# Row gathers held back at layer boundaries and in the closing of the hybrid recurrences, with changed weaving rates

## The chip, the cores and the metric

The kernel runs on one core of a Trainium2 chip. The metric is the device time of one execution in microseconds. A core has five engines with an instruction queue each, which work side by side and wait for each other through semaphores: PE (TensorE, matrix products and transposes), DVE (VectorE), ACT (ScalarE), POOL (GpSimd) and SP (SyncE, which issues transfers). Each engine runs its own instructions strictly in order, so an instruction that waits holds up all that stand behind it in its queue.

## What is computed

A block of a language model for 512 tokens of width 1024, in float32: a Mamba-2 layer, a layer of sliding-window attention with sinks, a hybrid mixer (a gated delta rule and an mLSTM, four heads each), cross attention to 256 memory tokens, and a feed-forward part that gives each token 128 of 16384 small experts. Each layer normalises its input and adds its output. Cut to the layers' frame and to the feed-forward part, which the change is about:

```
x = x + rmsnorm(mamba2_mixer(rmsnorm(x, w0), ...), p0)
x = x + rmsnorm(swa_sink_mixer(rmsnorm(x, w1), ...), p1)
x = x + hybrid_mixer(rmsnorm_2(x, norm_mix_w), ...)
x = x + memory_cross_attention(rmsnorm_2(x, norm_xa_w), rmsnorm_2(mem, norm_mem_w), ...)
x = x + peer_ffn(rmsnorm_2(x, norm_ffn_w), ...)
return rmsnorm_2(x, norm_final_w)

# in peer_ffn, for a block of 128 tokens, after the choice of 8 x 16 experts eb with gates gb:
u = jnp.take(u_table, eb, axis=0)
act = gelu(jnp.einsum('phkd,pd->phk', u, xb))
out = jnp.einsum('phk,phkd->pd', gb * act, jnp.take(v_table, eb, axis=0))
```

The hybrid mixer ends with a normalisation of each head's output and a gate, and then the product with w_out:

```
go = rmsnorm_2(go, gdn_norm_w) * silu(g_z)
mh = rmsnorm_2(mh, mlstm_norm_w) * sigmoid(m_o)
return concatenate([go, mh]) @ w_out
```

## The kernel before

The 512 tokens are worked on in two groups of two blocks of 128. Each group runs through the five layers. The feed-forward part is done in two ways. The second group's goes through all experts as dense products: phase G builds a matrix of gates while the first products with U run, and phase D has 128 steps, one for each of 128 slices of the experts, of a product with U and one with V. The first group's feed-forward is done by rows: for each of its 2 blocks, each of 2 tables (u, then v) and each of 128 chosen experts, one indirect transfer fetches one row of 1024 numbers for each of the 128 tokens. That makes 512 gathers of 512 KB.

One such gather is issued by POOL (L1946). DVE then does one instruction with it: a dot product for a row of u (L1967), or a product and sum into x for a row of v (L1973). Between a block's last u and its first v come gelu on ACT (L1971) and a product with the gates on DVE (L1972). Six buffers `gu` hold rows, and `take` works on a row when five newer ones have been issued. After a block's last v row follows its final normalisation (`final`, L1856 to L1863, with the power `finr`).

These rows have no place of their own. The second group's layers are written as a generator that yields between pieces of work, and `run` issues rows at the yields (L1894 to L1905). At each yield a budget `acc` grows by a rate that belongs to the layer, never above 3; for each whole unit of it a row is issued, that is one gather and one DVE instruction for an older row. The rows get a lower priority by 300 places (GOFF) than the code around them, and a scheduler sorts each engine's instructions by priority and by when they can run; in the layers a row is also tied not to stand ahead of the matmul that was last written (`behind`). What is left of the rows when phase G ends is spread over the steps of phase D: a step gets a share of the rows left by its weight, 2 for the first 94 experts and 1 for the later ones.

The places around the change:

- A layer's last product is `out_part(..., last=True)` (L618). It works on four column pieces c of both blocks: c = 0, 1 of both, then c = 2, 3 block by block. Each piece is 8 matmuls; then `end_evac` adds it to the residual on DVE (L646), squares it on ACT (L648), and, where a norm follows the layer, multiplies it by a weight (L650, on DVE or POOL).
- `post` (L601) then makes the norm's factor: a reduction (L607), `rstd`, which is an addition on DVE (`pv`, L458) and a power on POOL (`pr`, L460), a product (L612) and the update of x in two halves (L615).
- `norm_T` (L480) makes the next layer's input: sums (L493 or L496), `rstd` again (`nv` L458, `nr` on POOL L460), the scaled x (`xn`, L500), PE transposes (`tp`, L412) and evacuations of these (L510). No product of the next layer can start before its first transposes.
- In the hybrid layer `finish(b, f0)` closes four heads of a block: ACT squares, DVE reduces (L1372 to L1374), `rstd` (`ov` L458, on POOL `or` L460), POOL multiplies with the gate (L1376), DVE with the factor (L1378). `outT` transposes the result. The heads f0 = 4 (mLSTM) are closed first, behind the recurrence; the heads f0 = 0 (gated delta rule) are woven into the first half of the product with w_out, whose evacuations are L656.
- `rstd`'s power runs on POOL, in the same queue as the gathers.

The matmuls of all layers stand at L404 in a helper. In the second group the boundaries lie, in the profiled execution, at 1106 to 1122 us (mamba to swa), 1266 to 1284 (swa to hybrid), 1538 to 1556 (hybrid to cross) and 1630 to 1640 (cross to route, the choice of experts); the closing in the hybrid layer at 1475 to 1525. Gates are built from 1825 to 1947, dense steps run from there to 2576.

Of the kernel before, what the change touches and what calls it, by code (L numbers as in the profile page):

```python
# [146 lines left out]
SPLIT_R = [V]  # L147
SPLIT_D = [V]
SPLIT = {"A": SPLIT_A, "B": SPLIT_B, "R": SPLIT_R, "D": SPLIT_D}
RB = 1.0  # L150
RR = 0.5
RT = 1.793
RBS = 1.1
RBH = 1.1
RBX = 1.1
RG = 0.5
RATE = {"A": 0.0, "T": RT, "B": RB, "R": RR, "G": RG, "swa": RBS, "hybrid": RBH, "cross": RBX}
RAWB = 3
# [17 lines left out]
class Cat:  # L176


    def __init__(self, tiles):
        self.tiles, self.n = tiles, tiles[0].shape[1]  # L180
# [6 lines left out]
class Kern:  # L187
    PD = 2

    def __init__(self, ctx, tc, a, out, groups, stop=None):  # L190
        self.ctx, self.tc, self.nc, self.a, self.out = ctx, tc, tc.nc, a, out
        self.groups = groups
        self.stop = stop
        self.cnt = {}
        pool = lambda n, b, **k: ctx.enter_context(tc.tile_pool(name=n, bufs=b, **k))
        self.cp = pool("c", 1)
        self.xp = pool("xp", len(groups))
        self.wp = pool("wp", 2)
        self.hp = pool("hp", 1)
        self.pp = pool("pp", 2)  # L200
        self.gp = pool("gp", 2)
        self.stack = {}
        self.phase = "A"
        self.tail = None
        self.rows = None
        self.hook = None
        self.tab = ("", [], [])
        self.push("op")
        self.push("cl")
        self.mp = pool("mp", 2, space=PSUM)  # L210
        self.dp = pool("dp", 2, space=DRAM)
        self.lp = None
        self.order, self.full = [], []
        for gi in range(len(groups)):
            w = weight_order(gi == 0)
            self.order += w
            self.full += [gi == len(groups) - 1 and PARTS.get(n[0]) in FULL for n in w]
        self.order += DENSE_SEQ
        self.full += [s[0] == "U" and s[1] < PLAIN for s in DENSE_SEQ]
        self.wraw, self.wsp = {}, {}  # L220
        self.wpos = self.rpos = self.cpos = 0
# [258 lines left out]
    def norm_T(self, x, nb, wcol, keep=None, halo=None, ss=None, full=False, dst=None):  # L480
        nc = self.nc
        gt = nb * 128
        xt = self.op_tile([128, nb, D], "xn", "oh") if "op" in self.stack else self.sb([128, nb, D], "xn", bufs=1)
        xn = [xt[:, b, :] for b in range(nb)]
        with self.tc.high_priority(HP):
            for b in range(nb):
                s4 = self.sb([128, 4], "nss")
                if ss is None:
                    for c in range(2):
                        sl = slice(512 * c, 512 * c + 512)  # L490
                        nc.scalar.activation(xn[b][:, sl], x[:, b, sl], AF.Square, accum_out=s4[:, c:c + 1])
                    s1 = self.sb([128, 1], "ns1")
                    nc.vector.tensor_tensor(s1, s4[:, 0:1], s4[:, 1:2], op=ALU.add)  # L493
                else:
                    s1 = self.sb([128, 1], "ns1")
                    nc.vector.tensor_reduce(s1, ss[:, b, :], axis=AX.X, op=ALU.add)  # L496
                r = self.rstd(s1, 1, "n", 1.0 / D)
                for c in range(2):
                    sl = slice(512 * c, 512 * c + 512)
                    nc.vector.tensor_scalar(xn[b][:, sl], x[:, b, sl], r, None, op0=ALU.mult)  # L500
        if dst is not None:
            hh, hl = dst
        else:
            hh, hl = self.hT_open(gt, halo, full)
        with self.tc.high_priority(HP):
            for k in range(8):
                p = self.ps([128, gt], "tp")
                for b in range(nb):
                    self.tr(p[:, b * 128:(b + 1) * 128], xn[b][:, k * 128:(k + 1) * 128])
                nc.scalar.activation(hh[:, k, :], p, AF.Copy, scale=wcol[:, k:k + 1])  # L510
                if full:
                    continue
                nc.vector.scalar_tensor_tensor(hl[:, k, :], p, wcol[:, k:k + 1], hh[:, k, :].bitcast(F32),
                                               op0=ALU.mult, op1=ALU.subtract)
        if keep is not None:
            for b in range(nb):
                nc.gpsimd.tensor_tensor(keep[0][:, b, :], xn[b], keep[1], op=ALU.mult)
        if halo is not None and halo[1] is not None:
            for j in range(2):
                nc.gpsimd.tensor_copy(halo[1][j], self.hx[j][:, :, gt:gt + 4])  # L520
        return hh, hl
# [96 lines left out]
    def out_part(self, key, oT, nb, kh, k0, evac, last=False, done=None):  # L618


        for c in (0, 1) if last else range(4):
            u = self.W((key, kh, c))
            for b in range(nb):
                p = self.ps([128, 256], "mm")
                self.n_half(p, u, oT, b, k0, True, True)
                evac(b, c, p)
                yield
        if last:
            us = [self.W((key, kh, c)) for c in (2, 3)]
            for b in range(nb):  # L630
                for c in (2, 3):
                    p = self.ps([128, 256], "mm")
                    self.n_half(p, us[c - 2], oT, b, k0, True, True)
                    evac(b, c, p)
                    yield
                if done is not None:
                    done(b)
# [403 lines left out]
    def hybrid(self, gi, x, nb):  # L1041
# [317 lines left out]
        oT = self.oT(gt, self.is_full(gi, "ho"))  # L1359

        def finish(b, f0):
            fs = slice(f0, f0 + 4)
            if f0 == 4:
                ab = self.sb([128, 4], "dab")
                nc.vector.scalar_tensor_tensor(ab, den[:, b], -1.0, den[:, b], op0=ALU.mult, op1=ALU.max)
                nc.vector.tensor_tensor(ab, ab, floor[:, b], op=ALU.max)
                nc.vector.reciprocal(cf[:, b, fs], ab)
            c = cf[:, b, fs]
            jk = self.sb([128, 4, 128], "sq", tag="X")
            so = self.sb([128, 4], "so")  # L1370
            nc.scalar.activation(jk, mixed[b][:, fs], AF.Square)
            nc.vector.tensor_reduce(so, jk, axis=AX.X, op=ALU.add)  # L1372
            nc.vector.tensor_tensor(so, so, c, op=ALU.mult)
            nc.vector.tensor_tensor(so, so, c, op=ALU.mult)  # L1374
            r = self.rstd(so, 4, "o", 1.0 / 128)
            nc.gpsimd.tensor_tensor(mixed[b][:, fs], mixed[b][:, fs], gate[:, b, fs], op=ALU.mult)  # L1376
            nc.vector.tensor_tensor(c, c, r, op=ALU.mult)
            nc.vector.tensor_tensor(mixed[b][:, fs], mixed[b][:, fs], c[:, :, None].to_broadcast([128, 4, 128]), op=ALU.mult)  # L1378
            yield

        def outT(f0):
            for f in range(f0, f0 + 4):
                self.to_T([mixed[b][:, f, :] for b in range(nb)], oT[0][:, f, :], self.lo(oT, f),
                          self.gdncol if f < 4 else self.mlcol[:, f - 4:f - 3])
                yield
# [7 lines left out]
        side = chain(*[gdn(b) for b in range(nb)])  # L1393
# [4 lines left out]
        yield from self.weave_keep(g_proj("h_z", 0, AF.Silu), side, 2.0)  # L1398
        yield from self.weave(side, ml, 0.5)
        yield from outT(4)  # L1400
        if gi == 0:
            yield from self.memory_kv(2, "cacc", 3)
        fin = chain(*[finish(b, 0) for b in range(nb)], outT(0))
        yield from self.weave(self.out_part("h_o", oT, nb, 1, 4, self.acc_evac(xs)), fin, 1.0)
        self.xss = self.pp.tile([128, nb, 4], F32, name="xss", tag="xss", bufs=2)
        yield from self.out_part("h_o", oT, nb, 0, 0, self.end_evac(xs, self.xss, "P"), last=True)
        if gi == 0:
# [478 lines left out]
    def run(self):  # L1886
# [4 lines left out]
        side = None  # L1891
        for gi, (b0, nb) in enumerate(self.groups):
            x = self.load_x(gi) if gi else x0
            acc = 0.0  # L1894
            for _ in self.layers(gi, x, nb):
                ph = "T" if self.tail is not None else self.phase
                if ph == "B" and self.layer in RATE:
                    ph = self.layer
                acc = min(3.0, acc + RATE[ph])
                while side is not None and acc >= 1:  # L1900
                    acc -= 1
                    with self.tc.high_priority(GOFF[self.phase] if self.tail is None else TOFF):
                        if next(side, 0) == 0:
                            side = None
# [8 lines left out]
            elif gi < len(self.groups) - 1:  # L1913
                side = self.after(gi, x, nb)
# [142 lines left out]
```

## Time and profile before

| | us |
|---|---|
| median of three executions | 2600.91 |
| the three | 2602.40, 2600.91, 2598.08 |
| the profiled execution, its own time | 2595.71 |
| its span in the profile | 2593.7 |
| PE busy | 2376.1 (92%) |
| DVE busy | 1987.4 (77%) |
| ACT busy | 1170.7 (45%) |
| POOL busy | 1077.3 (42%) |

The mean granted clock of the profiled execution is 0.963 of full speed. The page of the profile lists, in its section on the costliest groups, 256 gathers of u rows on POOL (313.0 us together) and 256 of v rows (367.5), 256 products L1967 on DVE (318.4) and 256 L1973 (335.3).

How to read it: a share of busy time is a mean over stages with different limits, so the stages are read one by one. Of a stretch, the table of busy times tells which engine has no free time in it. Where PE has gaps, the timeline of PE tells how long each gap was and what ended it, and the timelines of DVE and POOL tell what stood ahead of the instruction that PE waited for. A bracket such as `[3.27 <-POOL pr L460]` behind a row says that the engine stood idle for 3.27 us before it, and what ended that.

### The profile page before, as it was taken

Reading aid. Unit: us, or ns where it says so; the run is one execution under the profiler, and the core shown is the slowest. Engines: PE = TensorE matmul, PEld = TensorE weight load, DVE = VectorE, ACT = ScalarE, POOL = GpSimd, SP = SyncE. Lnnn points to the kernel's source line nnn. Section 1 sums busy time; section 2 is a strip of 40 time slices with the busy share of each in tenths; the row PEclk is TensorE's granted clock in tenths of the full one; section 3 lists DMA queues with packets and bytes.
Section 4 is the critical chain, followed back from the end, with each engine's and each line's share of the span. In section 5 each row is a group of like instructions: output and inputs, shape, how many; then the busy total and the mean of one; then the engine's idle time right before and its main releaser. Section 6 shows DMA issues by size and latency. Waiting matters only on the chain.

```text
span 2593.7 us, 41054 instructions
## 1 busy us (share of the span) xinstructions
PE 2376.1 (92%) x14872; PEld 2134.6 (82%) x14872; DVE 1987.4 (77%) x3989; ACT 1170.7 (45%) x2406; POOL 1077.3 (42%) x910
## 2 busy tenths in 40 slices
PE   7999998998989899979799859999769999999997
PEld 7999898998988788868678848888658999999974
DVE  7787657757589887877698786794997777777776
ACT  6766566644545433333252312222565444444443
POOL 1112001231011776753568775324335555555552
PEclk9999999999989899989899979999999999999999
DMA  6555434325446999986888689877888888888874
GB/s 203 178 172 156 148 118 142 116 89 150 141 131 197 352 380 358 341 297 224 336 308 302 226 324 353 288 236 282 249 237 302 316 311 286 319 317 300 294 276 152
DMA packets 203962, 642.33 MB, mean 248 GB/s; under 512 B 21104, under 2 KB 53360, under 8 KB 202480
## 3 DMA queue, kind: packets, MB, share of 16 engines
q1 hardware_dynamic: 97216, 347.19, 40.1%
q0 software_dynamic: 73728, 268.47, 28.6%
q10 hardware_dynamic: 32816, 24.06, 2.9%
q8 instruction: 117, 1.92, 0.3%
q14 instruction: 85, 0.70, 0.1%
HBM read 621.74 MB, written 17.89 MB: 247 GB/s over the span
## 4 chain that ended last, share of the span: by engine, by line
PE 60%; DVE 20%; issue 6%; POOL 6%; DMA 5%; ACT 4%; ACTq 0%; POOLq 0%; DVEq 0%; SPq 0%
PE mm L404 37%; PE ax L404 17%; PE tp L404 3%; POOL gu L1946 3%; PE tp L412 2%; DVE x L1973 2%; DVE gu L1967 2%; DMA gu<-in_p_v,eid 2%; DVE wlo L379 2%; DVE cacc L532 1%; DVE o L1736 1%; DMA gu<-in_p_u,eid 1%; DVE q L1738 1%; DVE o L1743 1%; ACT whi L376 1%
## 5 line engine op out<-in xcount | busy, mean ns | idle before, releaser
L379 DVE TENSOR_TENSOR wlo<-wraw,whi 128x1024 fp32r<-128x1024 f32 x285 | 357.2, 1254 | 206.7 <-ACT whi L376 206.4
L1946 POOL DMA_INDIRECT gu<-in_p_v,eid x256 | 367.5, 1436 | 192.4 <-DVE x L1973 111.5
L1946 POOL DMA_INDIRECT gu<-in_p_u,eid x256 | 313.0, 1223 | 273.8 <-DVE gu L1967 171.7
L404 PE MATMUL mm<-hl,whi 128*128 128x256 f32 (+1 forms) x1376 | 392.0, 285 | 0.0
L376 ACT CAST whi<-wraw 128x1024 fp32r<-128x1024 f32 x285 | 298.9, 1049 | 183.9 <-PE mm L404 86.6
L1967 DVE SCALAR_TENSOR_TENSOR gu<-gu,hf 128x1024 f32<-128x1024 f32 x256 | 318.4, 1257 | 45.4 <-DMA gu<-in_p_u,eid 45.0
L1973 DVE SCALAR_TENSOR_TENSOR x<-gu,act,x 128x1024 f32<-128x1024 f32 x256 | 335.3, 1310 | 14.4 <-DMA gu<-in_p_v,eid 13.4
L404 PE MATMUL mm<-hh,whi 128*128 128x260 f32 (+1 forms) x1232 | 331.9, 345 | 2.7 <-DVE spp L563 1.5
L404 PE MATMUL mm<-hh,wlo 128*128 128x260 f32 (+1 forms) x1200 | 320.9, 340 | 4.1 <-DVE wlo L379 4.1
L404 PEld LDWEIGHTS mm<-hl,whi 128*128 128x128 f32 x1376 | 262.7, 191 | 5.0
L1809 POOL TENSOR_TENSOR w<-act,w 128x256 fp32r<-128x256 f32 x128 | 146.4, 1144 | 281.9 <-issue 218.1
L404 PEld LDWEIGHTS mm<-hh,whi 128*128 128x128 f32 x1232 | 237.4, 195 | 22.7 <-ACT hh L510 2.8
L404 PEld LDWEIGHTS mm<-hh,wlo 128*128 128x128 f32 x1200 | 232.8, 196 | 21.5 <-DVE wlo L379 5.0
L404 PE MATMUL mm<-dhh,wlo 128*128 128x256 f32 x752 | 211.7, 282 | 0.0
L404 PE MATMUL mm<-dhh,whi 128*128 128x256 f32 x752 | 209.8, 279 | 0.0
L404 PE MATMUL mm<-wlo,hh 128*128 128x256 f32 x656 | 176.6, 329 | 0.0
L404 PE MATMUL mm<-whi,hh 128*128 128x256 f32 x608 | 166.8, 328 | 0.4 <-ACT hh L510 0.4
L404 PE MATMUL mm<-whi,oh 128*128 128x256 f32 x560 | 147.5, 328 | 1.3 <-DVE ysb L646 1.1
L404 PE MATMUL mm<-hh,wraw 128*128 128x256 f32 (+1 forms) x608 | 147.1, 390 | 0.3 <-ACT act L1706 0.3
L1804 ACT CAST w<-act 128x256 fp32r<-128x256 f32 x128 | 52.2, 408 | 206.9 <-DVE act L1802 204.7
L404 PEld LDWEIGHTS mm<-dhh,whi 128*128 128x128 f32 x752 | 141.1, 188 | 4.0
L404 PEld LDWEIGHTS mm<-dhh,wlo 128*128 128x128 f32 x752 | 141.3, 188 | 0.0
(494 smaller groups left out, 5646.6 us busy)
## 6 DMA issues: line engine op xcount, KB each, us to landing
wraw<-in_w SPq DMA_DIRECT2D x238, 512.0 KB, 4.0
wraw<-in_p_v SPq DMA_DIRECT2D x78, 512.0 KB, 4.7
wraw<-in_p_ut SPq DMA_DIRECT2D x69, 512.0 KB, 4.6
whi<-in_w SPq DMA_DIRECT2D x55, 512.0 KB, 6.1
wlo<-in_w SPq DMA_DIRECT2D x55, 512.0 KB, 6.2
wrawd<-in_p_v SPq DMA_DIRECT2D x50, 512.0 KB, 4.8
wrawd<-in_p_ut SPq DMA_DIRECT2D x36, 512.0 KB, 4.4
gd<-gst ACTq DMA_DIRECT2D x32, 384.0 KB, 3.6
```

Of the source, the lines that this page charges most:

```text
L376: nc.scalar.copy(hi, raw)
L379: (nc.gpsimd if le == "P" else nc.vector).tensor_tensor(lo, raw, hi.bitcast(F32), op=ALU.subtract)
L404: inst = self.last = self.nc.tensor.matmul(out, lhsT, rhs, start=start, stop=stop, skip_group_check=True)
L412: return self.nc.tensor.transpose(out, in_, self.ident[:in_.shape[0], :in_.shape[0]])
L532: nc.vector.scalar_tensor_tensor(acc, ps[:, 1 + j:1 + j + gt], w[:, j:j + 1], acc, op0=ALU.mult, op1=ALU.add)
L1736: nc.vector.tensor_tensor(o1, self.iota4.rearrange("p i t -> p t i"), row(self.sTb[:, 0, :]), op=ALU.is_equal)
L1738: nc.vector.tensor_tensor(q, self.iota4, col(self.sTb[:, 1, :]), op=ALU.is_equal)
L1804: nc.scalar.copy(wt[:, 0:gt], act)
L1809: nc.gpsimd.tensor_tensor(wt[:, gt:2 * gt], act, wt[:, 0:gt].bitcast(F32), op=ALU.subtract)
L1946: self.behind(k.nc.gpsimd.indirect_dma_start(out=t, out_offset=None, in_=table, in_offset=bass.IndirectOffsetOnAxis(ap=self.res[b][0][:, s ...
L1967: self.behind(nc.vector.scalar_tensor_tensor(t, t, 1.0, self.hf[:, b, :], op0=ALU.mult, op1=ALU.mult, accum_out=acts[b][:, s:s + 1]))
L1973: self.behind(nc.vector.scalar_tensor_tensor(x[:, b, :], t, acts[b][:, s:s + 1], x[:, b, :], op0=ALU.mult, op1=ALU.add))
```

## The change

It does two things. It changes the four rates: mamba 1.0 to 0.95, swa 1.1 to 1.15, hybrid 1.1 to 1.05, cross 1.1 to 0.95. And it adds a flag `quiet`. While it is set, `run` issues no row, except in the first group's tail (phase "T"). It is set when a layer's last product reaches its pieces c = 2, 3, and cleared when the next layer's `norm_T` has issued its transposes; it is set in the second group's `finish`, cleared after the transposes of the mLSTM half, set again by the `finish` of the other half and cleared when the first half of the product with w_out is written. The budget goes on growing meanwhile, up to its cap of 3. The flag stops rows from being issued into the program at these yields; rows issued at earlier yields keep the place that the scheduler finds for them.

```diff
-RB = 1.0
+RB = 0.95
-RBS = 1.1
-RBH = 1.1
-RBX = 1.1
+RBS = 1.15
+RBH = 1.05
+RBX = 0.95
...
         self.rows = None
+        self.quiet = False
... norm_T, behind the transposes and their evacuations
+        self.quiet = False
         if keep is not None:
... out_part
         if last:
             us = [self.W((key, kh, c)) for c in (2, 3)]
+            self.quiet = True
... hybrid
         def finish(b, f0):
+            self.quiet = gi > 0
             fs = slice(f0, f0 + 4)
...
         yield from outT(4)
+        self.quiet = False
...
         yield from self.weave(self.out_part("h_o", oT, nb, 1, 4, self.acc_evac(xs)), fin, 1.0)
+        self.quiet = False
... run
-                while side is not None and acc >= 1:
+                while side is not None and acc >= 1 and not (self.quiet and ph != "T"):
```

Rows issued in each stage of the second group, as the two programs issue them:

| stage | before | after |
|---|---|---|
| mamba | 126 | 116 |
| swa | 62 | 61 |
| hybrid | 109 | 91 |
| cross | 35 | 28 |
| route | 41 | 44 |
| phase G | 34 | 34 |
| phase D | 110 | 143 |

That is 36 rows fewer in the four layers. In phase D an expert of the first 94 gets 1.02 rows in the mean before and 1.32 after, a later one 0.51 and 0.66.

How the order on the engines changes is shown at three places. In the changed file the lines stand one to six higher: L1952 is L1946, L1973 is L1967, L653 is L650, L649 is L646, L461 is L460, L1380 is L1376. A row that ends in x4 stands for four alike.

POOL at the boundary mamba to swa, before, where `gu` is a row's gather, L650 a piece's weight and `pr` the norm's power:

```order
157 L460 TENSOR_TENSOR gr<-gv,mhalf 128x2
158 L1946 DMA gu<-in_p_u,eid 128x1024 x4
159 L650 TENSOR_TENSOR ysb<-ysb,bcw 128x256 x2
160 L1946 DMA gu<-in_p_u,eid 128x1024
161 L650 TENSOR_TENSOR ysb<-ysb,bcw 128x256
162 L1946 DMA gu<-in_p_u,eid 128x1024
163 L650 TENSOR_TENSOR ysb<-ysb,bcw 128x256
164 L1946 DMA gu<-in_p_u,eid 128x1024 x4
165 L460 TENSOR_TENSOR pr<-pv,mhalf 128x1 x2
```

And after:

```order
158 L461 TENSOR_TENSOR gr<-gv,mhalf 128x2
159 L1952 DMA gu<-in_p_u,eid 128x1024 x3
160 L653 TENSOR_TENSOR ysb<-ysb,bcw 128x256
161 L1952 DMA gu<-in_p_u,eid 128x1024
162 L653 TENSOR_TENSOR ysb<-ysb,bcw 128x256
163 L1952 DMA gu<-in_p_u,eid 128x1024
164 L653 TENSOR_TENSOR ysb<-ysb,bcw 128x256 x2
165 L461 TENSOR_TENSOR pr<-pv,mhalf 128x1 x2
```

The four gathers ahead of the two `pr` are gone, and none stands between the last two L650.

POOL in the closing of the hybrid layer, before, from the last factors of the recurrence (L1316, L1309) over the gate products (L1376) and the powers `or` of the two halves to the fourth `or`:

```order
260 L1316 TENSOR_TENSOR qd<-qd,cte 128x256 x2
261 L1309 TENSOR_TENSOR dec<-dec,triu 128x256
262 L460 TENSOR_TENSOR finr<-finv,mhalf 128x1
263 L1376 TENSOR_TENSOR mixed<-mixed,hgate 128x512
264 L1946 DMA gu<-in_p_u,eid 128x1024
265 L1376 TENSOR_TENSOR mixed<-mixed,hgate 128x512
266 L1946 DMA gu<-in_p_u,eid 128x1024
267 L1376 TENSOR_TENSOR mixed<-mixed,hgate 128x512
268 L460 TENSOR_TENSOR or<-ov,mhalf 128x4
269 L1946 DMA gu<-in_p_u,eid 128x1024
270 L1376 TENSOR_TENSOR mixed<-mixed,hgate 128x512
271 L1946 DMA gu<-in_p_u,eid 128x1024 x2
```

```order
272 L460 TENSOR_TENSOR or<-ov,mhalf 128x4 x2
273 L1946 DMA gu<-in_p_u,eid 128x1024 x4
274 L460 TENSOR_TENSOR or<-ov,mhalf 128x4
275 L1946 DMA gu<-in_p_u,eid 128x1024 x20
276 L460 TENSOR_TENSOR nr<-nv,mhalf 128x1 x2
```

The same place after:

```order
260 L1319 TENSOR_TENSOR qd<-qd,cte 128x256
261 L1380 TENSOR_TENSOR mixed<-mixed,hgate 128x512
262 L1952 DMA gu<-in_p_v,eid 128x1024 x2
263 L1380 TENSOR_TENSOR mixed<-mixed,hgate 128x512 x2
264 L1952 DMA gu<-in_p_v,eid 128x1024
265 L461 TENSOR_TENSOR or<-ov,mhalf 128x4
266 L1380 TENSOR_TENSOR mixed<-mixed,hgate 128x512
267 L1952 DMA gu<-in_p_u,eid 128x1024 x3
268 L461 TENSOR_TENSOR or<-ov,mhalf 128x4
269 L1952 DMA gu<-in_p_u,eid 128x1024 x2
270 L461 TENSOR_TENSOR finr<-finv,mhalf 128x1
271 L461 TENSOR_TENSOR or<-ov,mhalf 128x4 x2
```

Block 0's `finr` moves from ahead of the closing products to behind the second `or`; gathers still stand among the products, two, one, three and two of them.

DVE at the boundary hybrid to cross, before, where L646 is the evacuation of one piece, `gu,act` a row's product, and L496, L458, L500 lead to the next layer's transposes:

```order
1943 L1967 SCALAR_TENSOR_TENSOR gu,act<-gu,hf 128x1024
1944 L646 TENSOR_TENSOR x<-mm,x 128x256
1945 L1967 SCALAR_TENSOR_TENSOR gu,act<-gu,hf 128x1024
1946 L646 TENSOR_TENSOR x<-mm,x 128x256
1947 L1967 SCALAR_TENSOR_TENSOR gu,act<-gu,hf 128x1024
1948 L496 TENSOR_REDUCE ns_15326<-xss 128x1
1949 L496 TENSOR_REDUCE ns_15335<-xss 128x1
1950 L1967 SCALAR_TENSOR_TENSOR gu,act<-gu,hf 128x1024
1951 L458 TENSOR_SCALAR nv<-ns_15326 128x1
1952 L458 TENSOR_SCALAR nv<-ns_15335 128x1
1953 L1967 SCALAR_TENSOR_TENSOR gu,act<-gu,hf 128x1024
1954 L500 TENSOR_SCALAR xn<-x,nr 128x512 x4
```

And after:

```order
1916 L649 TENSOR_TENSOR x<-mm,x 128x256
1917 L1973 SCALAR_TENSOR_TENSOR gu,act<-gu,hf 128x1024
1918 L649 TENSOR_TENSOR x<-mm,x 128x256 x4
1919 L497 TENSOR_REDUCE ns_15239<-xss 128x1
1920 L497 TENSOR_REDUCE ns_15248<-xss 128x1
1921 L459 TENSOR_SCALAR nv<-ns_15239 128x1
1922 L459 TENSOR_SCALAR nv<-ns_15248 128x1
1923 L501 TENSOR_SCALAR xn<-x,nr 128x512 x4
```

The last four evacuations follow each other, and no row stands between them and the scaled x.

## Rows read from the trace of the kernel before

**Rows 1.** The page, busy time of each engine and its share of the span.

```profile
PE 2376.1 (92%) x14872; PEld 2134.6 (82%) x14872; DVE 1987.4 (77%) x3989; ACT 1170.7 (45%) x2406; POOL 1077.3 (42%) x910
```

**Rows 2.** Busy us by stretch: PE, PEld, DVE, ACT, POOL, then clock, DMA share, GB/s.

```profile
900.00:950.00 50.00, 45.82 (x218) 40.09 (x217) 41.15 (x80) 16.50 (x40) 38.76 (x30) 0.91 1.00 384
...
1110.00:1120.00 10.00, 0.00 (x0) 0.00 (x0) 4.94 (x22) 2.72 (x8) 4.68 (x8) 0.50 0.71 266
...
1540.00:1550.00 10.00, 5.71 (x18) 4.13 (x16) 9.12 (x20) 2.55 (x10) 4.68 (x5) 0.83 1.03 417
...
2200.00:2250.00 50.00, 50.00 (x324) 45.41 (x323) 39.89 (x37) 23.89 (x37) 26.54 (x19) 1.00 0.90 325
...
2500.00:2550.00 50.00, 48.09 (x183) 31.64 (x181) 37.01 (x39) 20.39 (x30) 25.39 (x21) 1.00 0.69 233
```

**Rows 3.** PE's timeline at the boundaries: start, duration, engine, line, operation, idle before it.

```profile
1120.04 0.66 PE L412 MATMUL tp<-ident,xn 128*128 128x128 f32 x2 [14.07 <-DVE xn L500]
...
1281.73 0.66 PE L412 MATMUL tp<-ident,xn 128*128 128x128 f32 x2 [13.72 <-DVE xn L500]
...
1542.20 3.36 PE L404 MATMUL mm<-wraw,oh 128*128 128x256 f32 x8 [1.90 <-DVE x L646]
...
1553.69 1.39 PE L412 MATMUL tp<-ident,xn 128*128 128x128 f32 x4 [6.08 <-DVE xn L500]
...
1628.34 1.89 PE L404 MATMUL mm<-whi,oh 128*128 128x256 f32 x8
...
1635.30 0.66 PE L412 MATMUL tp<-ident,xn 128*128 128x128 f32 x2 [3.34 <-DVE xn L500]
```

**Rows 4.** PE's waits from 1470 to 1525: sum, times, longest.

```profile
PE tp L412 <- DVE mixed L1378: 18.0, 2, 11.4
```

**Rows 5.** DVE's timeline in a dense step.

```profile
2200.26 1.23 DVE L379 TENSOR_TENSOR wlo<-wrawd,whi 128x1024 fp32r<-128x1024 f32 x1 [0.94 <-ACT whi L376]
...
2207.55 1.27 DVE L1973 SCALAR_TENSOR_TENSOR x<-gu,act,x 128x1024 f32<-128x1024 f32 x1
```

**Rows 6.** POOL's timeline at the boundary mamba to swa.

```profile
1106.54 0.99 POOL L1946 DMA_INDIRECT gu<-in_p_u,eid  x1 [0.16 <-issue]
...
1110.74 0.94 POOL L1946 DMA_INDIRECT gu<-in_p_u,eid  x1 [0.30 <-issue]
1111.70 0.59 POOL L460 TENSOR_TENSOR pr<-pv,mhalf 128x1 f32<-128x1 f32 x1
```

**Rows 7.** POOL's timeline in a dense step, one gather.

```profile
2203.94 1.77 POOL L1946 DMA_INDIRECT gu<-in_p_v,eid  x1
```

**Rows 8.** DVE's timeline at the boundary mamba to swa.

```profile
1107.11 0.14 DVE L458 TENSOR_SCALAR pv<-pss 128x1 f32<-128x1 f32 x1
...
1112.33 0.21 DVE L612 TENSOR_SCALAR pr<-pr,gr 128x1 f32<-128x1 f32 x1 [3.27 <-POOL pr L460]
```

**Rows 9.** POOL's timeline at the boundary swa to hybrid.

```profile
1268.18 1.73 POOL L650 TENSOR_TENSOR ysb<-ysb,bcw 128x256 f32<-128x256 f32 x1
...
1273.86 0.59 POOL L460 TENSOR_TENSOR pr<-pv,mhalf 128x1 f32<-128x1 f32 x1
```

**Rows 10.** DVE's timeline at the boundary swa to hybrid, the last row ahead of block 1's update.

```profile
1276.15 1.27 DVE L1973 SCALAR_TENSOR_TENSOR x<-gu,act,x 128x1024 f32<-128x1024 f32 x1
```

**Rows 11.** DVE's timeline at the boundary hybrid to cross.

```profile
1551.25 0.20 DVE L458 TENSOR_SCALAR nv<-ns 128x1 f32<-128x1 f32 x2
...
1553.06 1.67 DVE L500 TENSOR_SCALAR xn<-x,nr 128x512 f32<-128x512 f32 x4 [0.46 <-POOL nr L460]
```

**Rows 12.** DVE's timeline in route.

```profile
1651.09 0.49 DVE L1522 MAX8 tv<-sc 128x8 f32<-128x128 f32 x2 [11.25 <-ACT sc L1570]
```

**Rows 13.** PE's waits in mamba's body, 835 to 1100: sum, times, longest.

```profile
PE ax L404 <- DVE m_h L817: 14.4, 7, 4.8
```

**Rows 14.** PE's waits while gates are built, 1825 to 1950.

```profile
PE ax L404 <- DVE o L1743: 21.1, 18, 3.1
```

**Rows 15.** ACT's timeline in swa, at the first block's switch from u to v.

```profile
1133.38 1.28 ACT L1971 ACT_TABLE_LOAD   x1
```

## The prediction

> **What bounds the kernel now.** I read the busy shares first: PE works 92% of the span, the next engine 77% [rows 1]. So a gain can only come from stretches where PE stands, and the table of busy times by stretch says which those are [rows 2]. In the dense expert part PE is busy 50.00 of 50 us at full clock and DVE 39.89: PE sets the time there. In mamba PE is busy 45.82 of 50 with the granted clock at 0.91, and DVE is often what it waits for. At the boundary mamba to swa PE does nothing for ten microseconds, and the clock stands at 0.50, the lower of its two levels.
>
> Next I read, in PE's timeline, the row after each such gap [rows 3]. Its bracket tells how long PE stood and for which engine: 14.07 us at mamba to swa, 13.72 at swa to hybrid, 1.90 and then 6.08 at hybrid to cross, 3.34 at cross to route, all for DVE. Two waits of 18.0 us together end on DVE's L1378 in the hybrid closing [rows 4]. That is some 57 us at the places that the change touches. Much of it is a serial chain that no row gather causes (evacuate, square, reduce, power, scale, normalise, transpose); the question is what share of it is queued behind rows. The prices of a row are 1.27 us on DVE (its product) [rows 5] and 0.94 us on POOL alone, or 1.77 beside busy DVE, for its gather [rows 6, 7].
>
> **The change part by part.** Counting the gathers issued in each stage gives before and after: mamba 126 and 116, swa 62 and 61, hybrid 109 and 91, cross 35 and 28, route 41 and 44, gate building 34 and 34, dense 110 and 143. So 36 leave the four layers, 3 go to route and 33 to the dense part. The rows that the flag holds back are made up for by at most three afterwards, since the budget is capped at 3.
>
> *Mamba to swa.* POOL issues gathers from 1106.54 on, the last begins at 1110.74, and only then, at 1111.70, comes the power `pr` [rows 6]. Its input `pv` was written by DVE at 1107.11 to 1107.25, and DVE then stands 3.27 us for `pr` at L612 [rows 8]. The order of after has no gather ahead of `pr`, and none between the last two L650. POOL was free at 1106.38 (0.16 before its first gather), and `pv` comes by then, since the DVE row ahead of it is gone too. `pr` moves from 1111.70 to 1106.39: **5.3 us**. All behind it up to the transposes is a chain of the same pieces. Floor 3.3 (the wait at L612 alone), ceiling 6.6 (one more row of 1.27).
>
> *Swa to hybrid.* The last L650 on POOL ends at 1269.91, `pr` starts at 1273.86 behind three gathers [rows 9]: 3.95 us. A row of 1.27 us stands on DVE at 1276.15 between block 0's update and the transposes [rows 10]; it goes, while one evacuation, 0.33 us, moves in. 3.95 + 1.27 - 0.33 = **4.9 us**; floor 2.4, ceiling 6.5, if a second DVE row ahead also counted.
>
> *Hybrid closing.* Here flag and order disagree. The order of after shows eight gathers from the first closing product to the third `or`, where before there were five: rows generated earlier are placed late. Against that, block 0's final normalisation (its power `finr` and DVE's L1862) leaves the closing products and lands behind them. Following both orders by hand with the durations of before, the first transposes come about 1 us sooner, the second 2.9, and then PE stands 2.7 for block 0's other half. Of the 18.0 us of waits [rows 4] I take **1 us**; from -4 (three extra gathers of 1.3 us ahead of an `or`) to +4 (2.9 and 1 both kept).
>
> *Hybrid to cross.* Before, each of the last four L646 on DVE stands behind a row; after, the last four follow each other and L496, L458 and L500 stand directly behind. Three terms. PE's wait of 1.90 at 1542.20 for an L646 goes. The same eight matmuls took 3.36 us, where eight take 1.89 at full clock [rows 3]: 1.47. From the last matmul's end at 1547.61 to the transposes was 6.08; what stays is one evacuation and reduction (about 0.8), L458 to L500 by way of POOL (1553.06 - 1551.25 = 1.81, [rows 11]) and 0.63 to the transpose: 3.2, so 2.8 go. Sum **6.2 us**; floor 2.8, ceiling 8.
>
> *Cross to route.* Of the 3.34 us [rows 3], two rows sit between the last evacuations. The last matmul ends at 1631.96; without rows the normalisation of block 0 is out some 0.9 us later: **2.4 us**, from 0 to 3.3. The three rows that route gets fall into DVE's idle 11.25 us there [rows 12]: nothing.
>
> *Mamba's body.* Ten rows fewer, four of them at the boundary. PE waits 14.4 us, in seven pieces, for DVE's L817 [rows 13]. Six rows free 7.6 us of DVE; I take a quarter, **2 us**, since most rows lie beside PE work; from 0 to 7.6.
>
> *The switch of a block from u rows to v rows.* Block 1's leaves gate building, where it makes the longest of 18 waits, 3.1 us where the others average (21.1 - 3.1) / 17 = 1.1 [rows 14]: **2 us**. Block 0's moves in swa from the projections to directly ahead of the first softmax on ACT; its table load of 1.28 us [rows 15] plus 0.3 for the function then lie in that chain: **-1.6 us**, from -3 to 0.
>
> *The dense part.* 28 of the 33 rows go to its steady experts: 1.02 per expert before, 1.32 after. One expert takes 5.6 us. DVE idles 0.94 us in each ahead of one product, waiting for ACT [rows 5], and a row takes 1.27, so the average third of a row (0.4 us) fits. DVE runs ahead of PE by a ring of buffers, so an expert with two rows, which overshoots by 0.3 us, is smoothed over its neighbours. POOL is busy 26.5 of 50 us. The DMA share is 0.90 at 325 GB/s; 0.3 x 0.524 MB per 5.6 us adds 28 GB/s, and the boundary stretch of hybrid to cross shows 417 GB/s [rows 2]. So **0** there. In the tail of V products PE is busy only 48.09 of 50 [rows 2]; five rows there cost between 0 and 1.27 each, and I take 0.15: **-0.7 us**.
>
> A rule of the Trainium skill speaks against this part. In this trace a gather takes 1.77 us on POOL in the dense part and 0.94 where DVE stands [rows 7, 6]: it waits for DVE. The Trainium skill, "SBUF — State Buffer", section "Who interferes with whom", says why: VectorE and GpSimd share a port pair as an exclusive lock, so gathers whose descriptors GpSimd writes starve behind VectorE. That would make the dense part the worst place for more rows, and is the mechanism of the second rival below; the 1.77 agrees with it, but POOL still idles 23.5 of 50 us. By the rule the sum would be that rival's; by POOL's idle time it stays as it is.
>
> The sum: 5.3 + 4.9 + 1 + 6.2 + 2.4 + 2 + 2 - 1.6 - 0.7 = 21.5 us. The profiled run took 2595.71 us, so 2574.2 in its terms; the median of before, 2600.91, lies 5.2 above that run, which gives 2579.4, said as **2579**. The floors add up to 3.3 + 2.4 - 4 + 2.8 + 0 + 0 + 0 - 3 - 6.4 = -4.9, the ceilings to 6.6 + 6.5 + 4 + 8 + 3.3 + 7.6 + 2 = 38; all floors at once are unlikely.
>
> **The rivals.**
>
> *Given back.* The boundaries get shorter, but the next layer then starts while its weights or three catch-up rows still hold DVE or DMA (1.03 share at hybrid to cross, [rows 2]), and half or more of the gain is lost: 8 us left, 2593. For it: DVE rows in that stretch themselves wait for their data. Against it: the clock stands at its lower level in the gaps, and a shorter gap gives some of that back.
>
> *Slower: the moved rows cost their full price.* Place: the dense part's DVE, or POOL, whose gathers wait for DVE there. If DVE's lead over PE is eaten up and each of 33 rows costs 1.27 us, that is 42 - 21.5 = +20: 2621. It decides from 21.5 / 33 = 0.65 us a row on. Against it: DVE has 10 of 50 us free and PE none; a third of a row per expert needs 0.4 of 0.94.
>
> *Not what it says.* Rows are placed late by the scheduler, and as in the hybrid closing they may stay in the boundaries: 0 to 5 us, 2598. Against it: the orders of after show three of five boundaries clean.
>
> *More.* The layers may be bound throughout by DVE and DMA, as mamba looks; then each of the 36 rows taken out gives 1.27 us: 46 us, 2555. Against it: PE is at 10.00 of 10 in many stretches there.
>
> **How the numbers follow.** Forecast (gain of 8 to 37 us, around 2579) 0.67; given back 0.13; slower 0.06; not what it says 0.05; more 0.09. A measurement of this kernel can tell about 0.2%, 5.2 us, from no change: faster means below 2595.7, slower above 2606.1. "Given back" is faster in two of three cases. Faster 0.67 + 0.09 + 0.09 = 0.85; same 0.04 + 0.05 = 0.09; slower 0.06. The range 2563 to 2596 takes the ceilings' sum (2600.9 - 38) below and a gain of 5 us above; it leaves out the slower rival, most of "more" and part of "not what it says", together 0.17.
>
> **What would show each step.** In the profile of after: PE's gap ahead of the first transposes falls from 14.07 to about 9, from 13.72 to about 9, from 6.08 to about 3 and from 3.34 to about 1; POOL's `pr` starts within 0.2 us of its input; two waits on L1378 still add up to some 15 us; the dense part keeps PE at 50.00 of 50, with DVE near 43 and DMA near 350 GB/s. I am wrong if PE shows gaps in the dense part, if the gaps shrink but mamba, swa or hybrid between them grow, or if the gaps do not shrink at all.

## The result and the profile after

The changed kernel takes 2563.18 us (median of five, 2560.91 to 2571.5) against 2602.37 before (2598.08 to 2603.39): the ratio is 0.9857, with a 95% interval of 0.9838 to 0.9875. The forecast was 2579, with a range of 2563 to 2596. The direction is right and the time lies inside the range by 0.2 us, at its lower end, but the gain is 39 us where 22 were forecast. The profiled run took 2561.23 us, 34.5 less than the profiled run of before, where the sum said 21.5. So 13 us are to be accounted for.

First the rows that answer to [rows 3, 4]: PE's timeline of the changed kernel at the boundaries and in the closing (start, duration, instruction, idle time before it).

```profile
1105.18 0.66 PE L413 MATMUL tp<-ident,xn 128*128 128x128 f32 x2 [7.67 <-DVE xn L501]
...
1261.10 0.66 PE L413 MATMUL tp<-ident,xn 128*128 128x128 f32 x2 [7.57 <-DVE xn L501]
...
1481.30 0.69 PE L413 MATMUL tp<-ident,mixed 128*128 128x128 f32 x2 [12.06 <-DVE mixed L1382]
1486.89 0.66 PE L413 MATMUL tp<-ident,mixed 128*128 128x128 f32 x2 [4.89 <-DVE so L1378]
...
1499.65 0.41 PE L413 MATMUL tp<-ident,mixed 128*128 128x128 f32 x2 [1.08 <-DVE mixed L1382]
...
1523.74 0.41 PE L413 MATMUL tp<-ident,xn 128*128 128x128 f32 x2 [2.70 <-DVE xn L501]
...
1602.53 0.41 PE L413 MATMUL tp<-ident,xn 128*128 128x128 f32 x2 [1.00 <-DVE xn L501]
```

The gaps ahead of the four first transposes fell from 14.07, 13.72, 6.08 and 3.34 to 7.67, 7.57, 2.70 and 1.00. In the closing 12.06 + 4.89 + 1.08 stand where 11.41 + 6.55 stood: nothing gained there. No gather stands in the gap from mamba to swa any more, as POOL's timeline shows: `pr` now waits for its input and not for gathers (compare [rows 6]).

```profile
1092.10 0.98 POOL L1952 DMA_INDIRECT gu<-in_p_u,eid  x1 [0.16 <-issue]
1093.10 1.64 POOL L653 TENSOR_TENSOR ysb<-ysb,bcw 128x256 f32<-128x256 f32 x2
1095.48 0.57 POOL L461 TENSOR_TENSOR pr<-pv,mhalf 128x1 f32<-128x1 f32 x1 [0.74 <-DVE pv L459]
...
1102.35 0.75 POOL L916 MEMSET va<- 128x780 f32 x1 [1.82 <-DVE inv L875]
1103.05 0.61 POOL L918 COPY kT<-a_kc 128x512 f32<-128x512 f32 x1
1103.61 0.39 POOL L919 COPY va<-a_vc 128x260 f32<-128x260 f32 x1
1103.97 0.55 POOL L461 TENSOR_TENSOR nr<-nv,mhalf 128x1 f32<-128x1 f32 x1
```

What is left of that gap is not the bare chain. The input of `nr`, `nv`, is written at 1102.46 to 1102.61, and `nr` starts only at 1103.97, behind swa's own MEMSET and two copies. These 1.4 us stood there before the change too, and no row gather is their cause.

Then the dense part, busy us of PE, PEld, DVE, ACT, POOL, then granted clock, DMA share and GB/s of a stretch of the changed kernel. It answers to the fourth of [rows 2]: PE has no free time, DVE went from 39.89 to 42.84 and POOL from 26.54 to 32.42.

```profile
2200.00:2250.00 50.00, 50.00 (x324) 45.47 (x323) 42.84 (x40) 24.23 (x36) 32.42 (x21) 1.00 0.90 316
```

So the gaps shrank as forecast or more, except in the closing, and the dense part took the rows. The 13 us show when the span is cut at the same instructions in both traces. Durations in us; the number of gathers that POOL ran in each stretch stands behind a stroke.

| stretch, cut at PE's instructions | before | after | gained | in the sum |
|---|---|---|---|---|
| start to mamba's first `dtv` product | 806.1 | 804.4 | 1.6 | - |
| mamba's body | 299.9 / 122 | 293.1 / 116 | 6.8 | 2 |
| gap mamba to swa | 14.1 / 4 | 7.7 / 0 | 6.4 | 5.3 |
| swa | 148.0 / 58 | 148.3 / 61 | -0.4 | -1.6 |
| gap swa to hybrid | 13.7 / 5 | 7.6 / 0 | 6.2 | 4.9 |
| hybrid up to its closing | 209.0 / 75 | 208.1 / 76 | 0.9 | - |
| closing to cross's first transposes | 63.0 / 29 | 54.5 / 15 | 8.5 | 7.2 |
| cross to route's first transposes | 81.6 / 40 | 78.8 / 28 | 2.8 | 2.4 |
| route, gates, dense, end | 958.4 | 956.2 | 2.2 | 1.3 |

The four boundary stretches came in some 4 us above the sum altogether. The largest single difference is mamba's body, 4.8 us. Its two rows, before and after:

```profile
806.08:1105.97 299.89, 283.23 (x1432) 249.50 (x1432) 251.53 (x505) 117.72 (x278) 204.57 (x165) 0.94 0.91 335
```

```profile
804.44:1097.51 293.07, 275.73 (x1432) 244.13 (x1432) 249.45 (x493) 117.84 (x280) 192.90 (x160) 0.97 0.91 334
```

The same work, 1432 entries of PE, keeps it busy for 7.5 us less, at a mean granted clock of 0.97 where it was 0.94, and PE's idle time did not shrink (16.7 and 17.3 us). The DMA share is 0.91 in both.

### The profile page after: what moved, and what is told of

It is laid out like the page before. It is cut to its first block, busy times and chain, and to the rows that moved or that the text cites. A ratio compares the mean times of both kernels' runs of the same rounds, so it can differ in the third digit from the quotient of the medians.

```text
span 2558.7 us, 41068 instructions
## 1 busy us (share of the span) xinstructions
PE 2360.9 (92%) x14872; PEld 2124.7 (83%) x14872; DVE 1993.0 (78%) x3989; ACT 1169.8 (46%) x2406; POOL 1080.9 (42%) x910
## 4 chain that ended last, share of the span: by engine, by line
PE 62%; DVE 20%; issue 6%; POOL 5%; DMA 4%; ACT 3%; ACTq 0%; POOLq 0%; DVEq 0%; SPq 0%
PE mm L405 39%; PE ax L405 17%; PE tp L405 3%; PE tp L413 3%; POOL gu L1952 2%; DVE gu L1973 2%; DVE wlo L380 2%; DVE o L1742 1%; DMA gu<-in_p_v,eid 1%; DVE cacc L534 1%; DMA gu<-in_p_u,eid 1%; DVE x L1979 1%; ACT whi L377 1%; DVE o L1749 1%; DVE q L1744 1%
## 5 line engine op out<-in xcount | busy, mean ns | idle before, releaser
L380 DVE TENSOR_TENSOR wlo<-wraw,whi 128x1024 fp32r<-128x1024 f32 x285 | 355.0, 1247 | 175.3 <-ACT whi L377 174.6
L1952 POOL DMA_INDIRECT gu<-in_p_u,eid x256 | 315.6, 1233 | 332.3 <-DVE gu L1973 231.8
L1952 POOL DMA_INDIRECT gu<-in_p_v,eid x256 | 381.0, 1488 | 138.0 <-DVE x L1979 71.1
L1973 DVE SCALAR_TENSOR_TENSOR gu<-gu,hf 128x1024 f32<-128x1024 f32 x256 | 323.0, 1279 | 37.5 <-DMA gu<-in_p_u,eid 37.3
L1979 DVE SCALAR_TENSOR_TENSOR x<-gu,act,x 128x1024 f32<-128x1024 f32 x256 | 342.4, 1337 | 11.6 <-DMA gu<-in_p_v,eid 9.6
```

Of the source, the lines that this page charges most:

```text
L380: (nc.gpsimd if le == "P" else nc.vector).tensor_tensor(lo, raw, hi.bitcast(F32), op=ALU.subtract)
L1952: self.behind(k.nc.gpsimd.indirect_dma_start(out=t, out_offset=None, in_=table, in_offset=bass.IndirectOffsetOnAxis(ap=self.res[b][0][:, s ...
L1973: self.behind(nc.vector.scalar_tensor_tensor(t, t, 1.0, self.hf[:, b, :], op0=ALU.mult, op1=ALU.mult, accum_out=acts[b][:, s:s + 1]))
L1979: self.behind(nc.vector.scalar_tensor_tensor(x[:, b, :], t, acts[b][:, s:s + 1], x[:, b, :], op0=ALU.mult, op1=ALU.add))
```

## The experiments

The theory to be tested is the prediction's: the gain comes from the **places**, rows that stood ahead of the boundary chains. Its rival is the **count**: a row costs about the same wherever it stands in the layers, and 36 fewer at 39 / 36 = 1.08 us each are the gain. All ratios are against the kernel before, run on the same chip. RB, RBS, RBH and RBX are the rates of mamba, swa, hybrid and cross.

**Same counts, other places.** Two kernels separate them. In the first the flag is ignored and rates give the counts of after; in the second the flag works and rates give the counts of before.

```diff
-                while side is not None and acc >= 1 and not (self.quiet and ph != "T"):
+                while side is not None and acc >= 1:
... rates RB 0.92, RBS 1.09, RBH 0.92, RBX 0.88
```

> The flag is ignored and the rates are lowered further (0.92, 1.09, 0.92, 0.88), so that each layer has as many rows as the changed kernel (116, 61, 91, 29; dense 144) but rows stand in the boundaries as before. Theory 'places' (the gain comes from rows that no longer stand ahead of the boundary chains): the 14.07 and 13.72 us gaps stay, only mamba's 6.8 us and the switch's 2 us are gained, about 2593 us. Theory 'counts' (every row out of the layers gives its price of about 1.1 us back, wherever it stood: 36 x 1.08 = 39): about 2563 us, as the changed kernel.

Measured: 2569.80 us, ratio 0.9896 (0.9875 to 0.9917): 27 us gained by the ratio, without the flag. The first two gaps stayed at 11.7 and 13.6 us, and mamba's body alone gave 10.5.

```diff
-RB = 0.95, RBS = 1.15, RBH = 1.05, RBX = 0.95
+RB = 1.03, RBS = 1.17, RBH = 1.27, RBX = 1.20
```

> The flag works, and the rates are raised (1.03, 1.17, 1.27, 1.20), so that each layer has as many rows as the kernel before (126, 62, 108, 35; dense 108). Theory 'places': most of the gain stays, 39 less mamba's 6.8 and a little for denser rows between the boundaries, about 2575 us, with gaps of some 7.6 us at the first two boundaries. Theory 'counts': no gain, about 2602 us.

Measured: 2591.59 us, ratio 0.9967 (0.9950 to 0.9984): 9 us gained by the ratio, with the flag and no row fewer in the layers. Both theories missed, "places" by more: of the change's 37 us by its ratio some 27 go with the count and 9 with the places, and the two add up. Yet the gaps did shrink in the second kernel (8.3 and 9.0 us at the first two boundaries, 51.8 from the closing to cross, 77.6 in cross), by 5.8 + 4.7 + 11.1 + 4.0 = 26 us. Most of it was lost again in the bodies, to which the same rows had moved. (The profiled execution took 2597.61 us, 6 above the median; in it all of the 26 us was lost again.) Its hybrid body, and that of before:

```profile
1280.95:1507.14 226.19, 197.75 (x1080) 172.78 (x1080) 188.40 (x320) 69.85 (x152) 168.78 (x146) 0.93 0.83 293
```

```profile
1281.73:1490.74 209.01, 193.53 (x1080) 168.11 (x1080) 172.51 (x290) 75.19 (x156) 148.06 (x128) 0.95 0.79 274
```

Eighteen more rows there (93 for 75) cost 17.2 us, four more in mamba's body 7.8.

**The closing.** One kernel leaves the flag out of the hybrid closing, a second also lowers the hybrid rate so that the counts are those of after.

```diff
         def finish(b, f0):
-            self.quiet = gi > 0
... and in the second kernel
-RBH = 1.05
+RBH = 0.94
```

> The changed kernel without the flag in the hybrid closing; 10 rows return to the hybrid layer (101), dense 132. If the closing's part of the flag is worth what the two traces differ by there once the boundary to cross is taken off (9.1 - 0.65 - 6.2 = 2.3 us): about 2565 us. Theory 'counts': 10 x 1.08 = 11 us more, about 2574 us.

Measured: 2569.79 us, ratio 0.9883 (0.9863 to 0.9903): 7 us more than after by the ratio, but with 10 rows more in the layer, between the two expectations.

> The changed kernel without the flag in the hybrid closing, and the hybrid rate lowered to 0.94 so that the hybrid layer has 91 rows as in the changed kernel; all other counts are the same too. If only the count matters in the hybrid layer: 2563 us, as the changed kernel. If rows in the closing cost more than rows in the layer's body (the stretch from the closing to cross was 6.8 us longer without the flag): 2566 to 2570 us.

Measured: 2564.71 us, ratio 0.9874 (0.9857 to 0.9891), against 2562.44 for the changed kernel in the same session. Its stretch from the closing to cross takes 56.9 us with 21 rows, 3 us more than the 53.8 of the changed kernel there, but the times differ by 2.3 us, which lies within the intervals: that the flag in the closing is worth anything beyond its count is not shown.

**The count in mamba's body.** The kernel before with one rate lowered:

```diff
-RB = 1.0
+RB = 0.85
```

> The kernel before with mamba's rate alone lowered, 1.0 to 0.85: 18 rows fewer in mamba (108), 17 more in the dense part, no flag. The prediction priced a row in mamba's body at a quarter to a third of its DVE time (6 rows for 2 us): 18 x 0.33 = 6 us, about 2593 us. If a row there costs its whole price, as the 13.5 us between the changed kernel and the one with lower rates suggest (12 rows, 1.12 us each): 18 x 1.12 = 20 us, about 2579 us.

Measured: 2574.01 us, ratio 0.9915 (0.9903 to 0.9927): 22 to 24 us for 18 rows, 1.2 to 1.3 us each. That is the whole price, about four times the 0.33 us a row that the sum took. Mamba's body took 279.3 us with 106 rows in it, 20.6 us less for 16 gathers:

```profile
804.86:1084.20 279.34, 271.68 (x1432) 241.21 (x1432) 234.83 (x470) 117.78 (x278) 176.96 (x149) 0.98 0.90 328
```

PE stands 7.7 us there, and stood 16.7 before; PE's own work takes 271.7 us, and took 283.2, at a clock of 0.98 for 0.94. So about half of what the rows cost is idle time. The other half goes with PE's slower clock: busy time times granted clock is the same in both, 283.2 x 0.94 and 271.7 x 0.98 both giving 266 us. The same from the other side, the changed kernel with mamba's rate put back to 1.0, beside a second run of the changed kernel:

> The changed kernel once more, beside the others on one chip, as their common reference and for a second profile: 2563 us. If mamba's body again takes about 293 us, the 6.8 us that it gained is the change's; the kernel without the flag in the closing, whose mamba is the same code, showed 300.3.

Measured: 2562.44 us, ratio 0.9868 (0.9850 to 0.9886). Mamba's body took 295.8 us, in the kernel with equal counts and no flag in the closing 293.2, and 300.3 in the other, whose profiled execution took 2582.52 us, 13 above its median. So the same code varies by 3 us, and by 7 with that execution. The 6.8 of the two traces comes from one pair of executions; over these four the gain of mamba's body has a mean of 4.3 us.

> The changed kernel with mamba's rate alone put back to 1.0: 6 rows more in mamba (122), 6 fewer in the dense part. By the prediction's price for mamba's body (2 us for these six): 2565 us. At the price that the run with mamba's rate alone showed (22 us for 18 rows, 1.2 us each): about 2570 us.

Measured: 2569.49 us, ratio 0.9896 (0.9879 to 0.9913), 7.1 us more than the changed kernel for six rows, and no time of the one reaches into those of the other. Mamba's body took 300.3 us with its 122 rows, as before the change 299.9. So the six rows were worth some 7 us and not 2.

**What a row costs there.** A row is a gather on POOL, a transfer of 512 KB and a product on DVE. One kernel shortens the product of the first block's u rows (all rows of mamba's body are such rows), a second their transfer as well. Both leave out most of these rows' numbers from the result.

```diff
+            n = 64 if b == 0 else D
-            ... scalar_tensor_tensor(t, t, 1.0, self.hf[:, b, :], ...
+            ... scalar_tensor_tensor(t[:, 0:n], t[:, 0:n], 1.0, self.hf[:, b, 0:n], ...
... and in the second kernel, for these rows
-            ... indirect_dma_start(out=t, out_offset=None, in_=table,
+            n = 64 if b == 0 and not v else D
+            ... indirect_dma_start(out=t[:, 0:n], out_offset=None,
+                                   in_=table.rearrange("e (a n) -> (e a) n", n=n),
```

> The changed kernel; the DVE product of the first block's u rows (all rows in mamba, the first ones in swa) works on 64 of 1024 columns, so this part of the first block's output is left out. Gathers and transfers stay. If a row's price in mamba is its DVE time: mamba's waits (17 us) and the lower clock's 12 us mostly go, about 2540 us. If it is POOL or the DMA (share 0.91 in mamba): no change, about 2563 us.

Measured: 2561.98 us, ratio 0.9868 (0.9854 to 0.9883), no change, though DVE's busy time in mamba's body fell from 249 to 141 us. DVE's busy time is not the price. What DVE saved it spent waiting: in mamba's body it stood 55.0 us for the rows' transfers, where it stood 15.2 in the changed kernel.

> As the kernel with the small DVE product, and the gathers of the first block's u rows fetch 64 of 1024 numbers (of other rows), 32 KB instead of 512. POOL still issues each. If the price is DVE time alone: the same time as the run with the small product, within 3 us. If the DMA carries part of it: 10 us or more below it.

Measured: 2547.74 us, ratio 0.9810 (0.9796 to 0.9824), 14 us less than with the small product alone. The two kernels' rows for mamba's body:

```profile
802.97:1092.70 289.73, 275.10 (x1432) 244.18 (x1432) 140.64 (x493) 118.94 (x280) 154.76 (x160) 0.96 0.90 337
```

```profile
803.70:1085.33 281.63, 271.41 (x1432) 240.90 (x1432) 138.38 (x493) 119.44 (x280) 155.45 (x160) 0.96 0.50 145
```

The DMA share falls from 0.90 to 0.50, and the body comes near to the 279 us that it reaches with 104 to 108 whole rows. Of the 8.3 us between the two profiled executions mamba's body has 8.1. So the transfers are most of what the rows beyond some 104 cost here. With the transfers cut to a sixteenth the body still does not get below 279 us, but PE's timeline tells why: all of PE's idle time in it, 10.2 us, is one wait.

```profile
865.99 0.69 PE L405 MATMUL ax<-m_h,abc 128*128 128x64 f32 x2 [10.22 <-POOL abc L778]
```

That L778 stands in POOL's queue behind 21 gathers, which run from 835.8 to 864.1 us; in the kernel with the small product alone the scheduler puts eight ahead of it, and the same matmuls wait 7.7 us, for DVE's L820. So in this kernel POOL's queue, by its order, sets what is left of PE's idle time. What sets it with whole rows is not shown.

**How far it goes.** Two kernels move more rows.

```diff
-RB = 0.95, RBS = 1.15, RBH = 1.05, RBX = 0.95
+RB = 0.85, RBS = 1.05, RBH = 0.95, RBX = 0.85
... and the second
+RB = 0.70, RBS = 0.85, RBH = 0.80, RBX = 0.70
```

> The changed kernel with all four rates 0.1 lower: 28 rows fewer in the layers (104, 56, 83, 25), 27 more in the dense part (170). Theory 'places': little more to gain, 2558 to 2563 us, since the boundaries are empty already, and the dense part still takes the rows beside PE. Theory 'counts': 28 x 1.08 = 30 us less, about 2533 us. If the dense part is full (its DVE was busy 42.8 of 50 us), each of the 27 rows costs up to 1.3 us there: 2580 us or more.

Measured: 2543.70 us, ratio 0.9791 (0.9770 to 0.9812). It is faster than both kernels: 17 to 20 us less than the changed one for 28 rows, about two thirds of the 30 that "count" asked for. Mamba's body is at 279.6 us; the other layers gave little.

> The changed kernel with rates of 0.70, 0.85, 0.80, 0.70: 72 rows fewer in the layers than the changed kernel (86, 46, 71, 21), 214 in the dense part, about 2.0 per steady expert. DVE was idle some 7 of 50 us there at 1.32 rows per expert, room for 0.6 more. If the dense part takes them beside PE: 44 rows more than the kernel with lower rates at 0.65 to 1.1 us each, 2495 to 2515 us. If DVE fills up there, PE shows gaps in the dense part, and the time is 2525 us or more.

Measured: 2556.05 us, ratio 0.9852 (0.9835 to 0.9869). The dense part is full. Its stretch, for the kernel with 170 rows there, and for the one with 214:

```profile
2200.00:2250.00 50.00, 50.00 (x323) 45.31 (x323) 45.41 (x41) 24.11 (x36) 34.80 (x24) 1.00 0.94 338
```

```profile
2200.00:2250.00 50.00, 50.00 (x321) 44.15 (x320) 49.68 (x44) 23.11 (x36) 43.36 (x28) 1.00 0.98 365
...
2350.00:2400.00 50.00, 48.40 (x310) 42.55 (x310) 47.40 (x43) 22.51 (x35) 40.77 (x26) 1.00 1.00 388
```

DVE reaches 49.7 of 50 us, PE waits for its L380 products (its waits from 1960 to 2430 stand below), and everything from route on takes 977.1 us where it took 957.9. In these 470 us PE runs 2914 entries where the kernel with 170 rows runs 2998, so it falls some 13 us behind. DVE is busy 456 of the 470 us (427 with 170 rows) and the DMA share is 1.00 (0.96). PE's waits name DVE, but whether DVE's time or the DMA fills up first was not told apart.

```profile
PE ax L405 <- DVE wlod L380: 4.5, 6, 1.2
PE ax L405 <- DVE wlo L380: 3.5, 5, 1.4
```

A last kernel takes rows from mamba above all:

```diff
+RB = 0.76, RBS = 1.05, RBH = 1.00, RBX = 0.85
```

> The changed kernel with rates of 0.76, 1.05, 1.0, 0.85: 93 rows in mamba, 56, 88, 25, and 176 in the dense part, whose DVE was busy 45.6 of 50 us with 170 rows and 49.7 with 214. Against the run with lower rates (2544 us): mamba with 11 rows fewer gives at most 5 us, as it did from 104 to 86 rows, hybrid and the dense part nothing: 2538 to 2544 us. If the dense part is full at 1.6 rows per expert: 2548 us or more.

Measured: 2544.93 us, ratio 0.9799 (0.9784 to 0.9815), the same as the kernel with all rates lower. Mamba's body took 279.6 us with 93 rows, as with 104.

## Why the prediction was right, and where it fell short

The number came out inside its range by 0.2 us, which is luck as much as foresight, and the split of the gain did not come out. Of the 21.5 us the sum gave 19.8 to the places, the four boundary stretches. There the traces show 24 us. But rows held back there cost much of that again in the bodies, unless they leave the layers: with the counts of before the flag is worth 9 us, and the counts alone give 27 without it.

**The boundaries.** Right in place and nearly in size. The forecasts for the gaps were 9, 9, 3 and 1 us; 7.7, 7.6, 2.7 and 1.0 came. The first two gains were taken too small by 1.1 and 1.3 us. At mamba to swa the sum moved `pr` only, but rows ahead of the last evacuations had held DVE, too: `pv` was written 1.1 us behind the end of PE's last product before, and 2.3 us ahead of it after. The ceilings of 6.6 and 6.5 counted one such row more. Hybrid to cross gained more than its ceiling of 8. The last 80 matmuls of the layer start at the first row of these, in the trace of before and of after:

```profile
1524.56 3.62 PE L404 MATMUL mm<-wraw,oh 128*128 128x256 f32 x16
...
1532.26 3.72 PE L404 MATMUL mm<-wlo,oh 128*128 128x256 f32 x16 [0.63 <-DVE x L656]
1536.14 1.99 PE L404 MATMUL mm<-wraw,oh 128*128 128x256 f32 x8 [0.16 <-DVE x L646]
1538.31 1.99 PE L404 MATMUL mm<-whi,oh 128*128 128x256 f32 x8 [0.18 <-DVE x L646]
```

```profile
1503.61 3.62 PE L405 MATMUL mm<-wraw,oh 128*128 128x256 f32 x16
...
1519.15 1.89 PE L405 MATMUL mm<-whi,oh 128*128 128x256 f32 x8
```

From there to the first transposes (1553.69 and 1523.74) it took 29.1 us and takes 20.1, a gain of 9.0 us where 6.2 were forecast. The waits of 0.63, 0.16, 0.18 and 1.90 all went, the last wait fell by 3.4 us, and the last four times eight matmuls took 1.89 us each.

**The closing.** As forecast, the flag cleared the program and not the order there. But the waits still add up to 18 us, not to some 15, and up to the same matmuls this stretch took 33.8 us and takes 34.4: the 1 us forecast did not come.

**Mamba's body.** This term failed by its size: 2 us for six rows, which measured some 7. The prediction saw what PE waited for, DVE's L817, priced a row by its DVE time and took a quarter of it, since rows lie beside PE's work. The short product shows that DVE's busy time was not the price, the short transfer that the transfer is much of it, and two runs give 1.2 us a row, near the 1.26 us of 512 KB at the 417 GB/s of [rows 2]. The first of [rows 2] had pointed at it: a DMA share of 1.00 at 384 GB/s. The share of the whole body says the same: 0.91 with 122 and 116 rows and 0.90 with 104, so that up to there the body shrank with its bytes; then 0.87 with 93 and 0.86 with 86. The prediction used that share to price the dense part and not this one. Its rival "more" had this mechanism for all 36 rows and came nearer (2555) than the forecast, but not as a rule: from 104 rows to 86 a row in mamba's body costs 0.3 us in the mean, and in the hybrid body 14 rows fewer (62 for 76) gained nothing.

**The dense part.** Right: 33 more rows cost nothing that shows, and neither did 60 (from route on 958.4, 956.2 and 957.9 us). The rival "slower" was wrong at 1.3 rows per expert, and at 2 PE's waits stood where it said, on DVE, with the DMA share at 1.00 beside it. POOL, the other place that it named, was busy 32.42, 34.80 and 43.36 of 50 us with 143, 170 and 214 rows, and no wait of PE in the dense steps names it. The second thing that the prediction did not see is how much of the gain hangs on this part: with the rows kept in the layers, the shorter gaps are worth 9 us and not 26. The rival "given back" names this: it comes true where the rows have nowhere else to go.

**The switch from u to v rows.** Block 0's was put at -1.6 us; swa grew by 0.4 us with three rows more. Block 1's was put at 2 us in gate building. Its wait of 3.1 us is gone, but PE's waits over 250 us there add up to 41.5 us after and 40.0 before, so that these 2 us do not show where they were expected.

**The rest.** The start to mamba, 1.6 us, holds no change of rows; with the spread of the same code above it tells nothing.

## What to carry to other kernels

Side work that is woven into a stage is priced by that stage's scarcest resource, which need not be the engine that the waiting instruction names. Here the DMA share of the stretch was the figure to read first, and the product on DVE second. Clearing a gap and moving the work that stood in it are two edits: price both, since the cleared work lands somewhere, and the best place is a stage where one engine has no free time and the engines that the side work needs have some. Such a place has an edge (here between 1.6 and 2.0 rows per expert), so measure one step beyond it.

## What the runs showed that was not expected

- The price of a row in mamba's body is steep and then flattens: the body took 307.7, 299.9, 293.1, 279.6, 279.6 and 274.6 us with 126, 122, 116, 104, 93 and 86 rows.
- About half of that price goes with the clock: PE's busy time for the same 1432 entries is 284.2 us at a mean granted clock of 0.93, and 268.8 at 0.99.
- Unchanged code in one stage varied by 7 us over four executions (293.1, 293.2, 295.8 and 300.3, the last in an execution that was slow for its kernel), with the granted clock between 0.97 and 0.94, so that one pair of traces does not price a stage to better than that.
